# Input sums at fixed steps, a shortened last norm, and two shared first outputs in a hybrid encoder step

## The chip, the cores and the metric

The kernel runs on one core of one Trainium2 chip. A core has TensorE (PE in the profile, its weight loads PEld), VectorE (DVE), ScalarE (ACT), GpSimd (POOL) and SyncE (SP), each with its own instruction queue that runs in order, and 16 DMA engines. The metric is the device time of one execution in microseconds; the time of a kernel is the median of its runs. Loads and stores are issued by SP, additions into memory by DMA from POOL.

## The reference

One layer on 576 tokens (512 prompt, 64 sample) of width 2048, in float32. Conditioning gives shifts, scales and gates; then one input projection, two kinds of attention, an output projection, a post-norm, a squared-ReLU MLP of width 8192 and the last post-norm. What matters here is the second half:

```python
x = layer_norm(ALPHA * x + g_a * jnp.einsum('bse,ed->bsd', mix, w_out), ln_mix_g, ln_mix_b)
u = (_norm(x) * (1.0 + sc_m) + sh_m).astype(x.dtype)
h = jnp.square(jax.nn.relu(jnp.einsum('bsd,df->bsf', u, w_up) + b_up))
x = layer_norm(ALPHA * x + g_m * jnp.einsum('bsf,fd->bsd', h, w_down), ln_mlp_g, ln_mlp_b)
```

The result also holds the keys, values and log forget values; the change does not touch them.

## The kernel before

Activations lie transposed: 128 partitions are 128 of the 2048 features, and a block row of `big`, `ahi` and `alo` is 16 such blocks by 576 tokens. Every float32 product is made as three reduced ones: an operand is split into a high part (a copy by ScalarE to the narrower type: `whi`, `shi`, `ahi`, `th`) and a low part (the difference, by VectorE: `wlo`, `slo`, `alo`, `tl`), and high x high, high x low and low x high are added. So each weight piece costs ScalarE one copy and VectorE one subtraction before TensorE can use it.

The order of work is written out by hand. `em` is the emitter: TensorE's loop calls `em.tick()` once per step (in a plain product a step is one input block, that is three matmuls; 16 steps are one output block), and a tick puts out whatever is due. `em.after(n, fn)` makes `fn` due n steps later; generators in `em.side` and `em.back` advance by one `yield` per step, one behind the other. `em.drain()` puts out all that is left at once. Since each engine's queue runs in order, the step at which an instruction is put out decides what it stands behind.

The tokens go in two groups: A is columns 256 to 576, B is columns 0 to 256. The stages that the change touches:

*Up blocks of group B.* After the mixer's post-norm, 12 of the 64 blocks of the up projection are made plainly (`up_block`, `proj`): 16 steps per block, the weights in pieces of half a block that SP loads to `raw` (three buffers, refilled when a piece's `wlo` is done), split two pieces ahead in `take()` (L160, L161). `up_block` ends in a relu on ScalarE (L1015), 3 steps later the square on VectorE (L1018), then a store `hd` by SP; for blocks 8 to 11 a negated copy `nrelu` on ScalarE (L1020) and its store `nd` follow. The remaining 52 blocks use sums of inputs and of weights, seven products in place of eight. The input sums are made beside group B's up blocks by the generator `input_sums`: for each of 8 pairs of feature blocks it loads the pair from `ud` to `x32` (L1054, two buffers, two pairs ahead), makes two differences at once (L1062), a third (L1064) and a fourth sum (L1066) in a tile `sums`, copies the high parts on ScalarE (L1070, L1071) and subtracts the low parts on VectorE (L1073, L1075). A pair takes 18 steps.

*The turn.* Behind the last up block come `Sums`: the weight pieces of the seven-product stages, loaded to `sraw`, added (`add`, L1108 to L1112) and split (`make`, L1128, L1129) four ahead. The old pools are closed, and the first `make(4)` stands before the first matmul.

*The end.* The last four hidden blocks are multiplied plainly for all 16 outputs: `down_last(k, cols)` makes outputs 2k and 2k+1 for the given token columns, in four steps each (`four_blocks`, L1324 to L1326), and `gated` adds them to `big`. All 16 are made for group A, then all 16 for group B with the kept weights. `stats` gathers mean and variance by transposes beside it. Group A's last norm, `final_norm`, runs beside group B's products: `ln_finish` makes mean and inverse root (a power on POOL) and spreads them by a matmul with a diagonal; then eight pairs of blocks are normalised (L1436: subtract, multiply), by VectorE for groups 2, 8 and 14 and by POOL for the others, scaled by ScalarE (`affine`, L1426) and stored (`y_out`, L1431). Group B's, `final_last`, stands at the very end.

The pools lie on a left and a right stack; a tile waits for the earlier tiles whose memory it takes.

Of the kernel before, what the change touches and what calls it, by code (L numbers as in the profile page):

```python
# [172 lines left out]
def program(tc, xT, cT, cr, wad0, wad1, bada, win0, win, wf, bf, rel, ck, cv, clogf, wout0, wout, wup, bup, wst, lnv,  # L173
# [3 lines left out]
    with ExitStack() as ctx:  # L177
# [832 lines left out]
        def up_block(f, cols):  # L1010
            ps = new_acc()
            proj(ahi, alo, cols, ps)
            (a, b), = cols
            r = rl.tile([P, NT], F32, tag="relu", name=f"relu{f}_{a}", bufs=2)[:, a:b]
            S.activation(r, ps[:, 0, : b - a], AF.Relu, bias=bupc[:, f : f + 1])  # L1015

            def square():
                V.tensor_tensor(r, r, r, ALU.mult)  # L1018
                if f in nd:
                    S.mul(n, r, -1.0)  # L1020

            if f in nd:
                n = rl.tile([P, NT], F32, tag="nrelu", name=f"nrelu{f}_{a}")[:, a:b]
            em.after(3, square)
            em.after(7, lambda: nc.sync.dma_start(hd[f][:, a:b], r))
            if f in nd:
                em.after(8, lambda: nc.sync.dma_start(nd[f][:, a:b], n))
# [18 lines left out]
        def input_sums():  # L1046


            xs = {}

            def load(p):
                if p < 8:
                    x = xs[p] = xt.tile([P, 4, HN], F32, tag="x32", name=fresh("x32"), bufs=2)
                    nc.sync.dma_start(x.rearrange("p (a b) c -> p a (b c)", b=2), ud[p])  # L1054

            load(0)
            load(1)
            yield from wait(12)
            for p in range(8):
                x = xs.pop(p)  # L1060
                t = xt.tile([P, 4, HN], F32, tag="sums", name=fresh("sums"))
                V.tensor_tensor(t[:, 0:2], x[:, 0:4:3], x[:, 1:2].to_broadcast([P, 2, HN]), ALU.subtract)  # L1062
                yield from wait(3)
                V.scalar_tensor_tensor(t[:, 2], t[:, 0], -1.0, x[:, 3], ALU.mult, ALU.subtract)  # L1064
                yield from wait(3)
                V.scalar_tensor_tensor(t[:, 3], t[:, 2], -1.0, x[:, 2], ALU.mult, ALU.subtract)  # L1066
                load(p + 2)
                yield from wait(1)
                h1, l1 = (v[:, 2 * p, HN:] for v in (ahi, alo))
                S.copy(h1, t[:, 0])  # L1070
                S.copy(th[:, p], t[:, 1:])  # L1071
                yield from wait(5)
                V.tensor_tensor(l1, t[:, 0], h1.bitcast(F32), ALU.subtract)  # L1073
                yield from wait(3)
                V.tensor_tensor(tl[:, p], t[:, 1:], th[:, p].bitcast(F32), ALU.subtract)  # L1075
                yield from wait(3)
# [4 lines left out]
        class Sums:  # L1081
# [33 lines left out]
            def make(self, upto):  # L1115
                while self.made < min(upto, self.n):
# [4 lines left out]
                    if q in self.places:  # L1121
                        hi, lo = self.places[q]
                    else:
                        hi, lo = (
                            self.pool.tile([P, 7, P], F32R, tag=t, name=f"{t}{q}", bufs=4)[:, : raw.shape[1]]
                            for t in ("shi", "slo")
                        )
# [25 lines left out]
        sums.pool_raw.append(srx.enter_context(tc.tile_pool(name="sr2", bufs=1, reuse_waits="tile")))  # L1153
        sums.load()

        swx = ExitStack()
        sw = swx.enter_context(tc.tile_pool(name="sw", bufs=1, side="right", reuse_waits="tile"))
        sums.pool = sw
        sums.make(4)
        z = sw.tile([P, 7, HN], F32, name="z")  # L1160
# [7 lines left out]
        UP, DOWN = (0, 2, 5, 4, 1, 6, 3), (1, 3, 6, 4, 2, 0, 5)  # L1168
# [237 lines left out]
        with tc.tile_pool(name="fl", bufs=1, side="right", reuse_waits="tile") as flp:  # L1406
# [13 lines left out]
            def affine(eng, g, a, b):  # L1420

                for kb in (g, g + 1):
# [16 lines left out]
            def final_norm(tiles, a, b):  # L1439

                yield from wait(6)
                yield from ln_finish(mp, stf, mur1, tiles, new_tr, EPS / ALPHA**2, 6)
                for g in range(0, KB, 2):
                    eng = V if g in (2, 8, 14) else G
# [3 lines left out]
                    affine(S, g, a, b)  # L1448
                    y_out(g, a, b)

            def final_last(tiles, a, b):
# [4 lines left out]
                dg = mp.tile([P, 2, n, P], F32, name="dg_last")  # L1456
                ps = new_acc()[:, :, : n * P]
# [5 lines left out]
                for j in range(2):  # L1463
                    for i in range(n):
                        V.tensor_scalar(dg[:, j, i], ident, mv[:, i, 0:1] if j == 0 else rs[:, i : i + 1], None, ALU.mult)
                    T.matmul(ps[:, j], ones, dg[:, j].rearrange("p a b -> p (a b)"), start=True, stop=True)
                    S.copy(mur[:, j], ps[:, j])
                mine, other = [0, 2, 6, 8, 12, 14], [4, 10]
                for g in other:
                    for _ in norm_pair(G, g, a, b, [mur[:, j] for j in range(2)]):  # L1470
                        pass
                    affine(G, g, a, b)
                work = [norm_pair(V, g, a, b, [ps[:, j] for j in range(2)]) for g in mine]
                next(work[0])
                for i, g in enumerate(mine):
# [3 lines left out]
                    affine(S, g, a, b)  # L1479
# [9 lines left out]
            for k in range(8):  # L1489
                down_last(k, GROUP_B)  # L1490
# [111 lines left out]
```

## Time and profile before

| | |
|---|---|
| time, median of 3 runs | 2587.33 us (2587.07 to 2587.91) |
| the profiled execution | 2590.35 us |
| its span | 2588.6 us |
| mean granted TensorE clock | 0.991 |
| TensorE busy | 2526.0 us, 98% |
| VectorE, ScalarE, POOL busy | 82%, 44%, 13% |
| DMA moved | 483.56 MB |
| up blocks of group B | 1154.8 to 1241.6 us |
| products and norms of the end | 2500 to 2588.6 us |

All times in the text are microseconds from the span's start. In the answers of the profile a row of instructions reads: start, duration, engine, line of the kernel, operation, written <- read, shape, count, and in brackets the idle time ahead of it and what ended it. A row of waits reads: engine, tile and line <- what it waited for: total, times, longest.

### The profile page before, as it was taken

How to read it: one execution, taken by the hardware profiler on the slowest of the kernel's cores; microseconds unless marked ns; L12 is line 12 of the kernel's file. 1: busy time of each engine (PE TensorE's matmuls, PEld its weight loads, DVE VectorE, ACT ScalarE, POOL GpSimd, SP SyncE). 2: the span in 40 equal slices, each digit the busy share in tenths (PEclk: the TensorE clock that was granted, in tenths of full speed). 3: DMA queues.
4: the chain of work that ended last, by engine and by line, in shares of the span. 5: the costliest groups of instructions: out<-in, count | busy, mean ns of one | idle time of the engine just before them, and what ended most of it. 6: DMA issues, size and time to landing. Idle time of an engine off the chain costs nothing.

```text
span 2588.6 us, 48474 instructions
## 1 busy us (share of the span) xinstructions
PE 2526.0 (98%) x19235; PEld 2481.8 (96%) x19235; DVE 2126.7 (82%) x3740; ACT 1133.0 (44%) x1787; POOL 328.1 (13%) x373
## 2 busy tenths in 40 slices
PE   7999999999999999998999999999999999999996
PEld 5899999999999999998999999999999999999996
DVE  5668989898899558876788888888788988888886
ACT  2243333333333424764444444444555555555552
POOL 0021121232332200000000000000011111111114
PEclk8999999999999999999999999999999999999998
DMA  9845667656666544667555444444866666666662
GB/s 368 326 145 181 238 208 232 217 197 219 200 207 218 184 144 159 212 190 236 160 161 157 132 136 144 146 145 140 268 170 176 181 165 173 177 172 155 192 170 74
DMA packets 188819, 483.56 MB, mean 187 GB/s; under 512 B 16728, under 2 KB 49304, under 8 KB 187568
## 3 DMA queue, kind: packets, MB, share of 16 engines
q1 hardware_dynamic: 167728, 456.57, 53.6%
q0 software_dynamic: 20864, 23.89, 6.0%
q8 instruction: 151, 2.47, 0.4%
q14 instruction: 76, 0.62, 0.1%
HBM read 408.07 MB, written 57.77 MB: 180 GB/s over the span
## 4 chain that ended last, share of the span: by engine, by line
PE 83%; DVE 5%; issue 4%; DMA 3%; POOL 3%; ACT 1%; SPq 0%; ACTq 0%; POOLq 0%; DVEq 0%
PE acc L222 18%; PE q L1176 13%; PE q L1177 13%; PE q L1175 13%; PE acc L224 9%; PE tr L1176 2%; PE tr L1177 2%; PE tr L1175 2%; DVE junk L770 1%; DMA ada<-in_wad 1%; PE acc L1325 1%; PE acc L1324 1%; PE acc L1326 1%; PE tr L443 1%; DVE wlo L161 1%
## 5 line engine op out<-in xcount | busy, mean ns | idle before, releaser
L1128 ACT CAST shi<-sraw 128x896 fp32r<-128x896 f32 (+1 forms) x448 | 416.7, 931 | 468.3 <-PE q L1176 283.4
L222 PE MATMUL acc<-ahi,whi 128*128 128x288 f32 (+2 forms) x2384 | 603.7, 303 | 3.7 <-ACT whi L160 2.9
L224 PE MATMUL acc<-ahi,wlo 128*128 128x288 f32 (+2 forms) x2384 | 583.0, 295 | 9.0 <-DVE wlo L161 9.0
L222 PE MATMUL acc<-alo,whi 128*128 128x288 f32 (+2 forms) x2384 | 582.6, 294 | 0.0
L1129 DVE TENSOR_TENSOR slo<-sraw,shi 128x896 fp32r<-128x896 f32 (+1 forms) x448 | 475.9, 1072 | 46.7 <-ACT shi L1128 40.7
L222 PEld LDWEIGHTS acc<-ahi,whi 128*128 128x128 f32 x2384 | 406.3, 189 | 14.7 <-issue 5.7
L224 PEld LDWEIGHTS acc<-ahi,wlo 128*128 128x128 f32 x2384 | 409.5, 188 | 11.0 <-DVE wlo L161 11.0
L222 PEld LDWEIGHTS acc<-alo,whi 128*128 128x128 f32 x2384 | 409.2, 189 | 0.5 <-DVE alo L957 0.2
L770 DVE CUSTOM_DVE_ANT_0 junk<-ada,cb 128x512 f32<-128x512 f32 x512 | 367.2, 717 | 36.7 <-DMA ada<-in_wad 25.9
L1177 PE MATMUL q<-ahi,slo 128*128 128x288 f32 x1296 | 383.2, 296 | 0.0
L1176 PE MATMUL q<-tl,shi 128*128 128x288 f32 x1296 | 383.0, 296 | 0.0
L1175 PE MATMUL q<-th,shi 128*128 128x288 f32 x1296 | 382.0, 295 | 0.4 <-DVE z L1192 0.4
L1176 PE MATMUL q<-alo,shi 128*128 128x288 f32 x1296 | 382.1, 295 | 0.0
L1175 PE MATMUL q<-ahi,shi 128*128 128x288 f32 x1296 | 381.2, 294 | 0.4 <-DVE z L1190 0.4
L1177 PE MATMUL q<-th,slo 128*128 128x288 f32 x1296 | 381.2, 294 | 0.0
L161 DVE TENSOR_TENSOR wlo<-raw,whi 128x1024 fp32r<-128x1024 f32 x208 | 256.7, 1237 | 104.4 <-ACT whi L160 103.1
L160 ACT CAST whi<-raw 128x1024 fp32r<-128x1024 f32 x208 | 216.9, 1047 | 117.5 <-PE acc L222 97.3
L1175 PEld LDWEIGHTS q<-th,shi 128*128 128x128 f32 x1296 | 243.9, 188 | 1.2 <-issue 0.8
L1175 PEld LDWEIGHTS q<-ahi,shi 128*128 128x128 f32 x1296 | 243.9, 188 | 0.7 <-DVE z L1190 0.7
L1176 PEld LDWEIGHTS q<-alo,shi 128*128 128x128 f32 x1296 | 244.1, 188 | 0.0
L1177 PEld LDWEIGHTS q<-th,slo 128*128 128x128 f32 x1296 | 243.9, 188 | 0.0
L1177 PEld LDWEIGHTS q<-ahi,slo 128*128 128x128 f32 x1296 | 243.7, 188 | 0.0
(299 smaller groups left out, 4045.9 us busy)
## 6 DMA issues: line engine op xcount, KB each, us to landing
sraw<-in_wst SPq DMA_DIRECT2D x232, 512.0 KB, 4.4
ada<-in_wad SPq DMA_DIRECT2D x192, 512.0 KB, 5.9
raw<-in_win SPq DMA_DIRECT2D x96, 512.0 KB, 4.4
raw<-in_wout SPq DMA_DIRECT2D x64, 512.0 KB, 3.7
hp<-z SPq DMA_DIRECT2D x26, 1008.0 KB, 6.9
raw<-in_wup SPq DMA_DIRECT2D x48, 512.0 KB, 4.4
big<-z POOLq DMA_DIRECT2D x74, 288.0 KB, 5.1
alo<-hp SPq DMA_DIRECT2D x34, 576.0 KB, 6.0
```

The lines of the kernel that those rows point to most:

```text
L160: nc.scalar.copy(hi, raw)
L161: nc.vector.tensor_tensor(lo, raw, hi.bitcast(F32), ALU.subtract)
L222: T.matmul(o, whi, x[:, kb, a:b], start=start and x is hi, stop=False, **kw)
L224: T.matmul(o, wlo, hi[:, kb, a:b], start=False, stop=stop, **kw)
L443: T.matmul(ps[32 * k : 32 * k + 32, : 2 * P], cst[:, 4 * i + k, :], raw[:, k, :], start=i == 0, stop=i == 3,)
L770: V.tensor_tensor_reduce(junk, raw[:, k], cb[:, v], 1.0, 0.0, ALU.mult, ALU.add, parts[:, 2 * l + k, v, q : q + 1],)
L1128: S.copy(hi, raw)
L1129: V.tensor_tensor(lo, raw, hi.bitcast(F32), ALU.subtract)
L1175: T.matmul(out, wh, xh, start=start, stop=False)
L1176: T.matmul(out, wh, xl, start=False, stop=False)
L1177: T.matmul(out, wl, xh, start=False, stop=stop)
L1324: T.matmul(out, w[0][:, j], hi[:, a:b], start=j == 0, stop=False)
```

## The change

- The negated copy of a relu goes from step 3 (behind the square) to step 9, its store from 8 to 12.
- `input_sums` is no generator any more: all its pieces are put out by `em.after` at fixed steps, a pair every 19. Pair p is loaded at step 19p-4, summed at 12, 14 and 16, copied at 25, and its low parts follow at 30 and 32. There are three `x32` tiles, and the sums are written over them (the third and fourth change places, hence `UP`).
- No drain ahead of the last up block; `sums.add` of the first weights is put out 13 steps into it. The split weights lie in one tile for high and low part, in other pools; the first split piece and `z` have a pool of their own.
- Group A's last norm starts without the 6 waits and with 3 in place of 6 in its finish; VectorE takes groups 2, 6 and 10.
- Group B's last norm has a tile and an accumulator each for mean and scale, the last pair's scaling is shared by ScalarE and VectorE, and the stores of POOL's groups come later.
- Outputs 0 and 1 of the last four blocks are made for both groups at once, with group A's.

```diff
             def square():
                 V.tensor_tensor(r, r, r, ALU.mult)
-                if f in nd:
-                    S.mul(n, r, -1.0)
...
             if f in nd:
-                em.after(8, lambda: nc.sync.dma_start(nd[f][:, a:b], n))
+                em.after(9, lambda: S.mul(n, r, -1.0))
+                em.after(12, lambda: nc.sync.dma_start(nd[f][:, a:b], n))
...
+            xs, todo = {}, []
+            for i in (0, 2, 1):
+                xt.tile([P, 4, HN], F32, tag=f"x32_{i}", name=fresh("x32"))
             for p in range(8):
...
+                def load(p=p):
+                    xs[p] = xt.tile([P, 4, HN], F32, tag=f"x32_{p % 3}", name=fresh("x32"))
+                    nc.sync.dma_start(xs[p].rearrange("p (a b) c -> p a (b c)", b=2), ud[p])
...
+                def fourth(p=p):
+                    x = xs[p]
+                    V.scalar_tensor_tensor(x[:, 2], x[:, 3], -1.0, x[:, 2], ALU.mult, ALU.subtract)
+
+                def high(p=p, h1=h1):
+                    S.copy(h1, xs[p][:, 0])
+                    S.copy(th[:, p], xs[p][:, 1:])
...
+                for n, fn in ((-4, load), (12, both), (14, third), (16, fourth), (25, high), (30, low1), (32, low3)):
+                    todo.append((max(19 * p + n, 0), len(todo), fn))
+            for n, _, fn in sorted(todo):
+                em.after(n + 1, fn)
...
-                        hi, lo = (
-                            self.pool.tile([P, 7, P], F32R, tag=t, name=f"{t}{q}", bufs=4)[:, : raw.shape[1]]
-                            for t in ("shi", "slo")
-                        )
+                        hl = self.pools[q % 4 > 0].tile([P, 2, 7, P], F32R, tag=f"shl_{q % 4}", name=f"shl{q}")
+                        hi, lo = (hl[:, i, : raw.shape[1]] for i in range(2))
...
-        em.side.append(input_sums())
+        input_sums()
         for f in range(FP):
             if f == FP - 1:
-                em.drain()
                 xtx.close()
...
                 sums.load()
                 sums.load()
+                em.after(13, sums.add)
             up_block(f, GROUP_B)
         em.drain()
-        sums.add()
...
-        UP, DOWN = (0, 2, 5, 4, 1, 6, 3), (1, 3, 6, 4, 2, 0, 5)
+        UP, DOWN = (0, 2, 6, 4, 1, 5, 3), (1, 3, 6, 4, 2, 0, 5)
...
             def final_norm(tiles, a, b):
-                yield from wait(6)
-                yield from ln_finish(mp, stf, mur1, tiles, new_tr, EPS / ALPHA**2, 6)
+                yield from ln_finish(mp, stf, mur1, tiles, new_tr, EPS / ALPHA**2, 3)
                 for g in range(0, KB, 2):
-                    eng = V if g in (2, 8, 14) else G
+                    eng = V if g in (2, 6, 10) else G
...
-                dg = mp.tile([P, 2, n, P], F32, name="dg_last")
-                ps = new_acc()[:, :, : n * P]
+                dg = [mp.tile([P, n, P], F32, name=f"dg_last{j}") for j in range(2)]
+                ps = [new_acc()[:, 0, : n * P] for _ in range(2)]
...
-                    affine(S, g, a, b)
-                    if i in (0, 3):
+                    affine((S, V if i + 1 == len(work) else S), g, a, b)
+                    y_out(g, a, b)
+                    if i in (1, 4):
                         y_out(other[i // 3], a, b)
-                    y_out(g, a, b)
 
             for k in range(8):
-                down_last(k, GROUP_A)
+                down_last(k, (*GROUP_A, *GROUP_B) if k == 0 else GROUP_A)
...
             for k in range(8):
-                down_last(k, GROUP_B)
+                if k > 0:
+                    down_last(k, GROUP_B)
```

More of the change, by code (lines that the diff above doesn't have):

```diff
@@ L1046, in input_sums @@
         def input_sums():
[L1049 to L1058, printed above, removed]
-            for p in range(8):
[L1060 to L1068, printed above, removed]
-                h1, l1 = (v[:, 2 * p, HN:] for v in (ahi, alo))
[L1070 to L1076, printed above, removed]
@@ L1147, in program @@
                 sums.load()
+                em.after(13, sums.add)
             up_block(f, GROUP_B)
         em.drain()
-        sums.add()
         rlx.close()
         wpx.close()
-        sums.pool_raw.append(srx.enter_context(tc.tile_pool(name="sr2", bufs=1, reuse_waits="tile")))
+        swx = ExitStack()
+        right = lambda name, x=srx: x.enter_context(tc.tile_pool(name=name, bufs=1, side="right", reuse_waits="tile"))
+        s3 = right("s3")
+        sums.pool_raw.append(right("sr2"))
+        sw = right("sw", swx)
+        sums.pools = [sw, s3]
+        z = sw.tile([P, 7, HN], F32, name="z")
         sums.load()
-        swx = ExitStack()
-        sw = swx.enter_context(tc.tile_pool(name="sw", bufs=1, side="right", reuse_waits="tile"))
-        sums.pool = sw
         sums.make(4)
-        z = sw.tile([P, 7, HN], F32, name="z")
         forms = [
@@ L1418, in down_last, with affine @@
                     gated(m, outs, cols)
-            def affine(eng, g, a, b):
-                for kb in (g, g + 1):
+            def affine(engs, g, a, b):
+                for kb, eng in zip((g, g + 1), engs):
                     zz = big[:, kb, a:b]
@@ L1447, in final_norm @@
                         yield
-                    affine(S, g, a, b)
+                    affine((S, S), g, a, b)
                     y_out(g, a, b)
@@ L1464, in final_last @@
                     for i in range(n):
-                        V.tensor_scalar(dg[:, j, i], ident, mv[:, i, 0:1] if j == 0 else rs[:, i : i + 1], None, ALU.mult)
-                    T.matmul(ps[:, j], ones, dg[:, j].rearrange("p a b -> p (a b)"), start=True, stop=True)
-                    S.copy(mur[:, j], ps[:, j])
+                        V.tensor_scalar(dg[j][:, i], ident, mv[:, i, 0:1] if j == 0 else rs[:, i : i + 1], None, ALU.mult)
+                    T.matmul(ps[j], ones, dg[j].rearrange("p a b -> p (a b)"), start=True, stop=True)
+                    S.copy(mur[:, j], ps[j])
                 mine, other = [0, 2, 6, 8, 12, 14], [4, 10]
@@ L1471, in final_last @@
                         pass
-                    affine(G, g, a, b)
-                work = [norm_pair(V, g, a, b, [ps[:, j] for j in range(2)]) for g in mine]
+                    affine((G, G), g, a, b)
+                work = [norm_pair(V, g, a, b, ps) for g in mine]
                 next(work[0])
@@ L1478, in final_last @@
                     next(work[i])
-                    affine(S, g, a, b)
-                    if i in (0, 3):
+                    affine((S, V if i + 1 == len(work) else S), g, a, b)
+                    y_out(g, a, b)
+                    if i in (1, 4):
                         y_out(other[i // 3], a, b)
-                    y_out(g, a, b)
             for k in range(8):
-                down_last(k, GROUP_A)
+                down_last(k, (*GROUP_A, *GROUP_B) if k == 0 else GROUP_A)
                 if k % 2 == 1:
```

10 lines of the change are left out of this document (added).

## The prediction

> **What bounds the kernel now.** I read the busy table of the page first, then busy times by stretches of time (columns: the stretch, its length, busy us and instructions of PE, PEld, DVE, ACT and POOL, granted clock, DMA share, GB/s), then the waits and the order of instructions in the stretches where TensorE is not full.
>
> ```profile
> PE 2526.0 (98%) x19235; PEld 2481.8 (96%) x19235; DVE 2126.7 (82%) x3740; ACT 1133.0 (44%) x1787; POOL 328.1 (13%) x373
> ```
> ```profile
> 1840.00:2400.00 560.00, 560.00 (x4230) 559.69 (x4229) 480.91 (x665) 307.39 (x466) 71.28 (x62) 1.00 0.66 175
> ...
> 2500.00:2572.00 72.00, 66.34 (x502) 64.81 (x501) 53.05 (x106) 18.38 (x36) 21.50 (x13) 0.98 0.26 74
> ```
> ```profile
> 1154.80:1241.60 86.80, 74.81 (x578) 71.47 (x576) 56.63 (x79) 41.89 (x61) 0.00 (x0) 0.96 0.70 220
> 1178.80:1230.20 51.40, 43.90 (x338) 41.46 (x337) 37.57 (x56) 25.66 (x36) 0.00 (x0) 0.97 0.72 225
> 1230.20:1241.50 11.30, 11.30 (x98) 11.29 (x96) 5.23 (x6) 4.16 (x7) 0.00 (x0) 1.00 0.43 132
> ```
>
> The reader is to see that the whole kernel is TensorE at full clock except in three places that the change touches: 1154.8 to 1241.6 (the up blocks of group B, beside which the input sums are made), the turn right after it, and the end from about 2566 on. No matmul is removed, so only idle time there can be won. The last row gives the free pace: 96 matmuls in 11.30 us are 0.118 us each, so one step (three matmuls) is 0.353 us and a block of 16 steps 5.65 us. Twelve blocks would be 67.8 us and take 86.8. Blocks 3 to 9 fill the middle row (seven blocks of 48 matmuls, 336 of its 338): 39.6 us at free pace, in 51.4, so 11.8 us are lost there; blocks 0 to 2 (1154.8 to 1178.8) lose 24.0 - 17.0 = 7.0; the last two, with the sums done, lose nothing.
>
> The waits between 1154 and 1246:
>
> ```profile
> DVE wlo L161 <- ACT whi L160: 21.1, 11, 2.3
> ACT th L1071 <- DVE sums L1066: 11.4, 8, 2.0
> ...
> PE acc L224 <- DVE wlo L161: 9.0, 10, 2.8
> DVE sums L1062 <- DMA x<-ud: 5.1, 1, 5.1
> ```
>
> and one turn of the wheel, from VectorE's and ScalarE's order of time:
>
> ```profile
> 1205.94 1.23 DVE L161 TENSOR_TENSOR wlo<-raw,whi 128x1024 fp32r<-128x1024 f32 x1 [2.29 <-ACT whi L160]
> ...
> 1211.17 0.46 DVE L1066 SCALAR_TENSOR_TENSOR sums<-sums,x 128x288 f32<-128x288 f32 x1
> 1213.92 1.23 DVE L161 TENSOR_TENSOR wlo<-raw,whi 128x1024 fp32r<-128x1024 f32 x1 [2.29 <-ACT whi L160]
> ```
> ```profile
> 1211.66 0.92 ACT L1071 CAST th<-sums 128x864 fp32r<-128x864 f32 x1 [1.56 <-DVE sums L1066]
> 1212.48 0.47 ACT L1015 ACTIVATE relu<-acc,bupc 128x256 f32<-128x256 f32 x1
> 1212.85 1.98 ACT L160 CAST whi<-raw 128x1024 fp32r<-128x1024 f32 x2
> ```
>
> VectorE works from 1205.94 to 1211.63, then stands 2.29 us: its next weight part needs whi, whi stands on ScalarE behind the copy th, and th, issued one step after the fourth sum, waits for that sum. The engines take turns instead of overlapping: 7.98 us for a block of 5.65. Neither is full (37.57 and 25.66 us of 51.4).
>
> **The change, part by part.**
>
> *Sums at fixed steps.* The copy now follows the fourth sum by 9 steps (3.2 us) and the first low part follows the copy by 5. VectorE may run 3.2 us late before ScalarE feels it, so the 2.29 us stand goes. What is late next? VectorE's own work: 37.57 us for these seven blocks with a pair every 18 steps; at 19 steps, with the sums a little under half of it, some 0.9 less, 36.7 us against 39.6. That fits. DMA work is 0.72 x 51.4 = 37.0 us: that fits too. ScalarE has the same copies, in place of a separate sums tile the sums are written over x, at the same number of elements: nothing. Moving the negated copy from step 3 to 9 and its store from 8 to 12 lets ScalarE pass the square that it waits for; it exists for four of the twelve blocks only, and the SP queue then meets a store whose source is ready: nothing. The loads are the cost. Before, pair p+2 was requested at the fourth sum of pair p, about 30 steps before its use; now a pair is requested 16 steps ahead, on the SP queue that also carries raw weights and hd stores:
>
> ```profile
> DMA to landing us min/median/max: 5.3/6.0/6.8
> ```
>
> This is for the eight x loads. 16 steps are 5.65 us; 6.0 and about 0.4 to issue are 6.4, so VectorE waits about 0.7 us with the next wlo behind it, seven times: 4.9 us. Its spare time is 39.6 - 36.7 = 2.9, so about 2.5 us of the wait reaches TensorE, since part of the spare time is not where it is needed. Blocks 3 to 9: 39.6 + 2.5 = 42.1, gain **9.3**. Bounds: 0 (the wheel only finds another partner) and 11.8 (free pace).
>
> *The first sum* keeps its place: load at step 1, use at step 13, in both kernels, so blocks 0 to 2 keep their 7.0. That the second load no longer goes out with it could bring the landing to the shortest, 5.3: at most 0.6. I take nothing.
>
> *The turn.*
>
> ```profile
> 1241.73 0.47 ACT L1015 ACTIVATE relu<-acc,bupc 128x256 f32<-128x256 f32 x1 [3.75 <-PE acc L224]
> ...
> 1242.69 0.42 ACT L1020 ACTIVATE nrelu<-relu 128x256 f32<-128x256 f32 x1 [0.49 <-DVE relu L1018]
> ...
> 1244.22 1.78 ACT L1128 CAST shi<-sraw 128x896 fp32r<-128x896 f32 x2 [1.10 <-DVE sraw L1112]
> 1245.21 0.61 PE L1175 MATMUL tr<-ahi,shi 128*128 128x288 f32 x1 [3.51 <-ACT shi L1128]
> ```
>
> The weight sums now come at step 13 of the last block, three steps (1.06 us) before its end, their loads at its start instead of behind the drained work. ScalarE's copy shi then stands only behind the negated relu (to 1243.11), not behind the sums (1244.22): TensorE restarts **1.0** us earlier, with a gap of 2.5 instead of 3.51. The first shi tile lies in the new layout on raw weights that are long split, so it waits for no store. Bounds: 0 (sraw lands late) and 1.0, without the clock.
>
> The clock is the open part:
>
> ```profile
> 1171.00:1174.00 3.00, 2.21 (x13) 2.22 (x14) 1.43 (x3) 1.41 (x2) 0.00 (x0) 0.76 0.36 115
> 1174.00:1177.00 3.00, 3.00 (x20) 3.00 (x19) 2.52 (x3) 1.76 (x3) 0.00 (x0) 0.67 0.96 295
> ...
> 1246.00:1249.00 3.00, 2.72 (x12) 2.67 (x12) 2.92 (x6) 1.17 (x2) 0.00 (x0) 0.50 0.50 175
> 1249.00:1252.00 3.00, 3.00 (x17) 3.00 (x16) 2.93 (x5) 1.03 (x2) 0.00 (x0) 0.65 0.50 145
> 1252.00:1255.00 3.00, 3.00 (x25) 3.00 (x24) 2.79 (x5) 1.47 (x2) 0.00 (x0) 1.00 0.44 106
> ```
>
> After the turn 29 matmuls pass in 6 us instead of 50: 21 x 0.12 = 2.5 us lost. But the longest wait of PE above, 2.8 us, comes just ahead of the first two of these rows, and there the clock fell to 0.76 and 0.67 as well. A gap of 2.5 lies near that, so I give nothing. The Trainium skill, "TensorE: Matmul & The Clock Gate", section "Why this matters for your kernels", says that idle gaps up to about 3 us between bursts leave the clock up; by it the turn would gain 3.5 instead of 1.0. This case's 2.8 us gap speaks against it, so it has a small chance below.
>
> *The middle* (split weights hi and lo in one tile, other addresses): same instructions under a TensorE that is full (560.00 of 560): nothing, bounds -1 and +1.
>
> *The end.*
>
> ```profile
> 2553.43 19.00 POOL L1436 TENSOR_TENSOR big<-big,mur 128x640 f32<-128x640 f32 x10 [8.95 <-ACT mur L323]
> 2572.53 0.70 POOL L1462 TENSOR_TENSOR rs_last<-rs_last,mhalf 128x2 f32<-128x2 f32 x1
> ```
> ```profile
> 2566.04 3.39 DVE L1436 TENSOR_TENSOR big<-big,mur 128x640 f32<-128x640 f32 x2
> ...
> 2576.72 7.26 DVE L1436 TENSOR_TENSOR big<-big,acc 128x512 f32<-128x512 f32 x12 [2.98 <-ACT mur L1467]
> ```
> ```profile
> 2575.06 1.22 PE L1466 MATMUL acc<-dg_last,ones 128*128 128x256 f32 x2 [0.95 <-ACT mur L1467]
> ```
> ```profile
> L1431 SPq DMA_DIRECT2D out_yT<-big x16: 372/373/429, 2558.5 to 2585.5; - x16
> ```
>
> Group A's norm on POOL ends at 2572.43, and the power for group B's last norm stands behind it in the same queue: that sets the end. Group A's products end later by two blocks of twelve 256-wide matmuls, 24 x 0.118 = 2.8 us. The norm then starts earlier by the 6 waits removed and by 12 within its finish (6 + 6 + 6 + 6 steps become 3 + 3 + 3 + 3): 18 x 0.353 = 6.4. Net 3.6 earlier: the ten operations, still ten and beside the same six VectorE ones, run 2549.9 to 2568.9. VectorE's pair of 3.39 us moves from the last place (group 14) to group 10, ahead of group B's end, so its statistics are ready by then too. From POOL's end to VectorE's norm it is 4.3 us now (2572.43 to 2576.72), because mean and scale share one accumulator and the first subtraction waits for both. With two accumulators it needs only the mean: 1.22 for the matmul and, as an estimate from ScalarE's 0.42 for a 256-wide copy, 0.5 for the two 128-wide diagonals, about 1.8. Start 2570.7 instead of 2576.7: 6.0. The last affine pair shared by ScalarE and VectorE saves one of ScalarE's, about 0.5. POOL's own two pairs end about when VectorE's last does, and their store goes ahead of it. Gain **6.5**; bounds 3.5 (only POOL's start counts) and 7.5. Products of the first two outputs for both groups are the same matmuls: nothing.
>
> Sum: 9.3 + 1.0 + 6.5 = 16.8. The profiled span 2588.6 becomes 2571.8, its execution of 2590.35 becomes 2573.5; the runs' median, 3.0 below that execution, becomes **2570.5**.
>
> **The rivals.**
>
> 1. *Only the end is won.* The wheel finds a new partner (raw weight buffers that come free late), blocks 3 to 9 keep 51.4. For it: three raw buffers, each refilled only after a wlo. Against: DMA has 37.0 us of work in 51.4. Gain 1.0 + 6.5: **2579.8**.
> 2. *Free pace, and the clock kept at the turn*: 11.8 + 3.5 + 6.5 = 21.8, **2565.5**. For it: VectorE's 36.7 of 39.6. Against: 6.0 us landings on 5.65 us notice.
> 3. *Slower: each x load stalls as the first does now.* The first costs TensorE 2.8 us and then 16 matmuls of slow clock (33 instead of 56 from 1171 to 1177, less 0.79 us idle), 1.9 us: 4.7. Seven more are 32.9 against the 11.8 lost now: 21.1, less 7.5, is 13.6 slower, **2600.9**. It decides from (11.8 + 7.5) / 7 = 2.8 us a load; that needs a landing near 8.5 us, and the longest seen is 6.8.
> 4. *No change*: the sums win nothing and POOL's end does not move, because the doubled first blocks push group A back as far as the waits bring it forward; only the turn is left, 1.0 at most: **2586.3**.
>
> **How the numbers follow.** Forecast (2564 to 2577) 0.60, rival 1 0.15, rival 2 0.13, rival 4 0.07, rival 3 0.05. About 0.2% (5.2 us) is what a measurement of this kernel can tell from no change. Faster: 0.60 + 0.15 + 0.13 = 0.88; same 0.07; slower 0.05. All bounds at their best (11.8, 0.6, 3.5, 1, 7.5) make 24.4 and 2562.9; the range 2563 to 2580 reaches from there over the forecast and rivals 1 and 2 and leaves out the 0.12 of the others.
>
> **What would show it.** Right: blocks of 5.7 to 6.3 us in the input-sum stage, hardly a wait of wlo on whi, VectorE's waits now on x loads; a gap of about 2.5 us at the turn; POOL's ten norm operations ending before 2569 less what was won earlier, and VectorE's last norm within 2 us behind. Wrong: blocks that stay at 7 to 8 us, x loads with waits over 2 us, or POOL still 3 us behind group B's statistics.

## The result, and the profile after

The changed kernel takes 2575.03 us (median of 5 runs, 2574.03 to 2579.54); the kernel before, 2587.91 in the same comparison. The ratio is 0.9948 (95% interval 0.9937 to 0.9959), a gain of 12.9 us, between 10.6 and 16.3 by the interval. Forecast were 2570.5 and a gain of 16.8, with a range of 2563 to 2580. The profiled execution took 2578.5 us, its span 2576.8, that is 11.8 less than the profiled span before.

The busy table of the changed kernel, then its busy times by stretches (columns as in the prediction):

```profile
PE 2522.5 (98%) x19235; PEld 2480.1 (96%) x19235; DVE 2125.9 (83%) x3741; ACT 1133.2 (44%) x1786; POOL 328.3 (13%) x373
```
```profile
1154.07:1233.65 79.58, 71.58 (x578) 69.70 (x576) 55.32 (x79) 40.38 (x58) 0.00 (x0) 0.98 0.73 240
```
```profile
1177.72:1220.65 42.93, 40.91 (x338) 39.89 (x337) 32.02 (x46) 23.26 (x31) 0.00 (x0) 1.00 0.79 260
1220.65:1233.65 13.00, 11.58 (x98) 11.33 (x96) 8.88 (x13) 5.11 (x9) 0.00 (x0) 1.00 0.54 192
```

The same matmuls, and the 12 up blocks of group B in 79.58 us instead of 86.71: blocks 3 to 9 in 42.93 instead of 51.40, but the last two in 13.00 instead of 11.30. The waits between 1150 and 1250:

```profile
ACT whi L160 <- DMA raw<-in_wup: 14.2, 8, 3.3
DVE x L1061 <- DMA x<-ud: 11.8, 5, 4.8
DVE wlo L161 <- ACT whi L160: 10.4, 8, 3.5
...
ACT th L1073 <- DVE x L1069: 6.7, 5, 1.7
PE acc L224 <- DVE wlo L161: 6.6, 6, 2.6
ACT nrelu L1025 <- DVE relu L1018: 4.6, 2, 2.6
ACT nrelu L1025 <- DMA nd<-nrelu: 4.5, 3, 3.2
```

The main reading rests on one more pair of rows, ScalarE's wait ahead of each pair's two copies, before (between 1154 and 1246) and after:

```profile
ACT ahi L1070 <- DVE sums L1062: 24.2, 8, 6.1
```
```profile
ACT ahi L1072 <- DVE x L1061: 3.8, 3, 1.4
```

This wait for the sums fell from 24.2 to 3.8 us, that of `wlo` for `whi` from 21.1 to 10.4, that of `th` for the fourth sum from 11.4 to 6.7; the wait for x grew from 5.1 (once) to 11.8 (five times). ScalarE now also waits for a DMA that was in no row before: `nrelu` for its own last store. The x waits one by one, and the landing of the eight loads:

```profile
1168.22 0.76 DVE L1061 TENSOR_TENSOR x<-x 128x576 f32<-128x576 f32 x1 [4.80 <-DMA x<-ud]
...
1182.59 0.76 DVE L1061 TENSOR_TENSOR x<-x 128x576 f32<-128x576 f32 x1 [1.63 <-DMA x<-ud]
...
1199.22 0.76 DVE L1061 TENSOR_TENSOR x<-x 128x576 f32<-128x576 f32 x1 [2.64 <-DMA x<-ud]
...
1212.21 0.76 DVE L1061 TENSOR_TENSOR x<-x 128x576 f32<-128x576 f32 x1 [1.40 <-DMA x<-ud]
...
1221.18 0.76 DVE L1061 TENSOR_TENSOR x<-x 128x576 f32<-128x576 f32 x1 [1.35 <-DMA x<-ud]
```
```profile
DMA to landing us min/median/max: 5.9/6.8/7.5
```

The turn, by ScalarE's, VectorE's and TensorE's order of instructions, and the clock after it:

```profile
1235.24 0.42 ACT L1025 ACTIVATE nrelu<-relu 128x256 f32<-128x256 f32 x1 [0.92 <-DMA nd<-nrelu]
1235.57 1.76 ACT L1134 CAST shl<-sraw 128x896 fp32r<-128x896 f32 x2
```
```profile
1233.17 0.69 DVE L1116 TENSOR_TENSOR sraw<-sraw 128x512 f32<-128x512 f32 x1 [2.41 <-DMA sraw<-in_wst]
...
1234.70 0.42 DVE L1018 TENSOR_TENSOR relu<-relu 128x256 f32<-128x256 f32 x1
```
```profile
1236.54 0.61 PE L1181 MATMUL tr<-ahi,shl 128*128 128x288 f32 x1 [2.73 <-ACT shl L1134]
```
```profile
1237.00:1240.00 3.00, 2.72 (x12) 2.37 (x12) 2.93 (x5) 1.16 (x2) 0.00 (x0) 0.50 0.59 175
1240.00:1243.00 3.00, 3.00 (x14) 3.00 (x14) 2.92 (x6) 1.02 (x3) 0.00 (x0) 0.50 0.44 127
1243.00:1246.00 3.00, 3.00 (x24) 3.00 (x23) 2.82 (x4) 1.03 (x2) 0.00 (x0) 0.95 0.33 117
```

The gap is 2.73 us instead of 3.51, and the clock behind it is as low as before. The end, by POOL and VectorE, with one row of the beginning of that stretch:

```profile
2543.50 19.16 POOL L1442 TENSOR_TENSOR big<-big,mur 128x640 f32<-128x640 f32 x10 [4.05 <-ACT mur L323]
2562.76 0.69 POOL L1467 TENSOR_TENSOR rs_last<-rs_last,mhalf 128x2 f32<-128x2 f32 x1
```
```profile
2564.26 7.33 DVE L1442 TENSOR_TENSOR big<-big,acc 128x512 f32<-128x512 f32 x12 [0.29 <-ACT mur L1472]
2571.63 0.41 DVE L1434 TENSOR_SCALAR big<-big,lnc 128x256 f32<-128x256 f32 x1
```
```profile
2511.18 1.30 DVE L288 BATCH_NORM_STATS2 stt<-tr 128x6 f32<-128x512 f32 x2 [1.56 <-DMA big<-z]
```
```profile
2511.93 0.66 PE L287 MATMUL tr<-ident,big 128*128 128x128 f32 x4 [1.43 <-DVE stt L288]
```

POOL's ten operations end at 2562.66, VectorE's last norm starts 1.6 us behind them (4.3 before). Group B's mean and variance were ready at 2561.67, so POOL now holds the last norm up by a microsecond at most. The last two rows are a wait that was not there before: group A's statistics wait for a DMA that reads `z`, and TensorE stands 1.43 us for them.

For all kernels below two lengths are compared, each read from one profile: *up to the turn*, from the first matmul of group B's up blocks to the first seven-product matmul, and *the end*, from the first plain 320-wide product of the last blocks to the end of the span. Ratios are to the kernel before, in the same comparison, with 95% intervals.

| kernel | ratio | up to the turn, us | end, us |
|---|---|---|---|
| before | 1 | 90.39 | 84.53 |
| changed | 0.9948 (0.9937 to 0.9959) | 82.47 | 80.31 |
| e1_sums_only | 0.9980 (0.9971 to 0.9989) | 84.09 | 84.61 |
| e9_last_norms | 0.9984 (0.9976 to 0.9993) | 90.36 | 79.29 |
| e2_end_only (changed, products apart) | 0.9975 (0.9963 to 0.9987) | 83.36 | 81.91 |
| e3_copy_at_17 | 0.9974 (0.9963 to 0.9984) | 86.77 | 79.93 |
| e4_load_early | 0.9950 (0.9936 to 0.9964) | 79.59 | 79.99 |
| e5_sums_later | 0.9938 (0.9925 to 0.9950) | 77.11 | 80.49 |
| e6_stats_off_z | 0.9947 (0.9935 to 0.9959) | 81.31 | 79.09 |
| e8_apart_off_z | 0.9950 (0.9936 to 0.9963) | 81.60 | 79.26 |
| e10_two_nrelu | 0.9936 (0.9924 to 0.9948) | 77.09 | 80.17 |
| e14_negated_at_3 | 0.9962 (0.9950 to 0.9975) | 83.97 | 79.79 |
| e13_together | 0.9934 (0.9922 to 0.9947) | 75.52 | 79.16 |
| e12_without_pool | 0.9919 (0.9906 to 0.9933) | 73.47 | 78.63 |

An interval is some 6 us wide, so effects of 1 to 3 us are read from the two lengths. Where the code is the same they agree within 0.7 us at the end (79.8 to 80.5 in the six kernels that have the change's) and within 2 up to the turn (82.47, 83.36, 81.31 and 81.60 in the change, e2, e6 and e8). Shorter pieces vary more: in these four, blocks 3 to 9 take 42.45 to 45.60 us and the gap at the turn is 2.69 to 3.32 us; the code of before has a gap of 3.51 us in its own profile and of 4.61 in that of e9_last_norms. The middle, 1259 us of the same work, varied between 1258.1 and 1261.8 without order, so the 1.1 us by which it is longer after the change says nothing.

### The profile page after: what moved, and what is told of

The parts are those of the page before. It is cut to its first block, busy times and chain, and to the rows that moved or that the text cites. A ratio compares the mean times of both kernels' runs of the same rounds, so it can differ in the third digit from the quotient of the medians.

```text
span 2576.8 us, 48159 instructions
## 1 busy us (share of the span) xinstructions
PE 2522.5 (98%) x19235; PEld 2480.1 (96%) x19235; DVE 2125.9 (83%) x3741; ACT 1133.2 (44%) x1786; POOL 328.3 (13%) x373
## 5 line engine op out<-in xcount | busy, mean ns | idle before, releaser
L1134 ACT CAST shl<-sraw 128x896 fp32r<-128x896 f32 (+1 forms) x448 | 416.7, 931 | 482.8 <-PE q L1183 310.3
L1135 DVE TENSOR_TENSOR shl<-sraw,shl 128x896 fp32r<-128x896 f32 (+1 forms) x448 | 476.2, 1073 | 51.6 <-ACT shl L1134 46.2
L1182 PE MATMUL q<-alo,shl 128*128 128x288 f32 x1296 | 384.6, 297 | 0.0
L1181 PE MATMUL q<-th,shl 128*128 128x288 f32 x1296 | 383.6, 296 | 0.5 <-DVE z L1198 0.4
L1182 PE MATMUL q<-tl,shl 128*128 128x288 f32 x1296 | 382.8, 295 | 0.0
L1183 PE MATMUL q<-ahi,shl 128*128 128x288 f32 x1296 | 382.7, 295 | 0.0
L1183 PE MATMUL q<-th,shl 128*128 128x288 f32 x1296 | 382.4, 295 | 0.0
L1181 PE MATMUL q<-ahi,shl 128*128 128x288 f32 x1296 | 381.2, 294 | 0.0
L1181 PEld LDWEIGHTS q<-th,shl 128*128 128x128 f32 x1296 | 244.0, 188 | 1.4 <-issue 0.9
L1183 PEld LDWEIGHTS q<-ahi,shl 128*128 128x128 f32 x1296 | 244.5, 189 | 0.0
L1181 PEld LDWEIGHTS q<-ahi,shl 128*128 128x128 f32 x1296 | 244.4, 189 | 0.0
L1183 PEld LDWEIGHTS q<-th,shl 128*128 128x128 f32 x1296 | 244.4, 189 | 0.0
L1182 PEld LDWEIGHTS q<-tl,shl 128*128 128x128 f32 x1296 | 244.1, 188 | 0.0
```

Of the source, the lines that this page charges most:

```text
L1134: S.copy(hi, raw)
L1135: V.tensor_tensor(lo, raw, hi.bitcast(F32), ALU.subtract)
L1181: T.matmul(out, wh, xh, start=start, stop=False)
L1182: T.matmul(out, wh, xl, start=False, stop=False)
L1183: T.matmul(out, wl, xh, start=False, stop=stop)
```

## The experiments

**The fixed steps alone.** The kernel before with the new `input_sums` and the moved negated copy; turn and end stay as they were.

```diff
-        em.side.append(input_sums())
+        input_sums()
...
-                em.after(8, lambda: nc.sync.dma_start(nd[f][:, a:b], n))
+                em.after(9, lambda: S.mul(n, r, -1.0))
+                em.after(12, lambda: nc.sync.dma_start(nd[f][:, a:b], n))
```

> The kernel before with the input sums at fixed steps (and the negated copy at step 9) alone. Theory (in the changed kernel the stage of group B's up blocks fell from 86.7 to 79.5 us, because ScalarE's copy no longer stands one step behind the fourth sum): the stage falls by 7 us, the turn and the end stay (gap about 3.6 us, end 84.5 us from the first plain product on), so 7 us faster than before, ratio about 0.9973. Rival (the drain removed ahead of the last up block and the early weight sums are part of that gain): 4 us or less.

Ratio 0.9980, 5.2 us. In the profile the twelve blocks take 79.02 us, 7.7 less than before and as in the change, so what this stage won is the steps' doing. The time is between the theory's 7 us and the rival's 4. The gap at the old turn is longer than in the profile before (3.51):

```profile
1234.17 0.61 PE L1183 MATMUL tr<-ahi,shi 128*128 128x288 f32 x1 [4.91 <-ACT shi L1136]
```

The old turn does its loads, adds and splits behind the last block, so part of what the stage wins may be spent there; one profile doesn't show it, since the same turn had a gap of 4.61 us in e9_last_norms. Against 84.09 us here, 81.3 to 83.4 with the change's code: by these profiles the new turn is worth 0.7 to 2.8 us once the stage is fast, which is little above the spread.

**The last norms alone.** The kernel before with the new `final_norm`, `affine` and `final_last`.

```diff
-                yield from wait(6)
-                yield from ln_finish(mp, stf, mur1, tiles, new_tr, EPS / ALPHA**2, 6)
+                yield from ln_finish(mp, stf, mur1, tiles, new_tr, EPS / ALPHA**2, 3)
...
-                    eng = V if g in (2, 8, 14) else G
+                    eng = V if g in (2, 6, 10) else G
```

> The kernel before, with the new last norms alone (final_norm without its six waits and with three steps instead of six, six of its norm operations on VectorE at groups 2, 6, 10, two accumulators and the shared affine in final_last); the first two outputs of the last blocks stay apart for the two token groups. Theory: with no doubled products group A's statistics come 2.8 us earlier than in the changed kernel, POOL's ten operations end near 2566 on the scale of the profile before, the end is then set by group B's own statistics, and the end stretch falls from 84.5 to 80 or 81 us; time 3.5 to 4.5 us less than before. Rival: POOL still ends behind group B's statistics, end stretch 81 to 82 with POOL's power directly behind its last norm operation. Rival: the end is not set by POOL at all, end stretch stays at 84 to 85, time as before.

Ratio 0.9984, 4.1 us; the end falls from 84.53 to 79.29.

```profile
2546.41 19.19 POOL L1436 TENSOR_TENSOR big<-big,mur 128x640 f32<-128x640 f32 x10 [3.61 <-ACT mur L323]
2569.31 0.70 POOL L1461 TENSOR_TENSOR rs_last<-rs_last,mhalf 128x2 f32<-128x2 f32 x1 [3.71 <-DVE rs_last L1460]
```

POOL is done at 2565.6 and then waits 3.71 us for group B's statistics: it no longer sets the end. Theory met, a little better than its 80 to 81. From here group B's own statistics set it, so a POOL that is done still earlier would win nothing more here.

**The doubled products undone.** The next kernel is the changed one with the first two outputs of the last blocks made for the groups apart, all else as in the change. The text on record under this label speaks of another kernel, the one that e9_last_norms is, and by that run it is missed: POOL ended 6.7 us earlier (6.4 expected), but the gain was 4.1 us and not 6.5 to 7.

```diff
-                down_last(k, (*GROUP_A, *GROUP_B) if k == 0 else GROUP_A)
+                down_last(k, GROUP_A)
```

> The kernel before with the two last norms changed (waits, engines, two accumulators, shared last scaling), but the products of the two groups kept apart. Theory (POOL's end and the shared accumulator set the end; the doubled outputs only push group A back): POOL ends 6.4 us earlier than before, group B's statistics then come last, VectorE's last norm starts about 2570.3 instead of 2576.7, 6.5 to 7 us faster, ratio about 0.9974. Rival (the doubled outputs are needed for the gain): 4 us or less.

```profile
2505.86 1.30 DVE L288 BATCH_NORM_STATS2 stt<-tr 128x6 f32<-128x512 f32 x2 [2.53 <-DMA big<-z]
```

The wait for the DMA that reads `z` grows from 1.56 to 2.53 us and the end from 80.31 to 81.91. So the doubled products, which put group A's first statistics later, cover part of this wait. The ratio, 0.9975, is 7 us from the change's; the two lengths show 2.5 of it. The profiled execution, 2576.28 us, was the fastest of its seven (median 2581.59), so the lengths come from one that lost less than most; where the others lost the rest is not known. The next two kernels ask what the wait is for, and whether covering it is all that the doubled products do.

```diff
-            mp, stf, mur1 = ln_tiles(flp)
+            mp, mur1 = flp, flp.tile([P, 2, NT], F32, name="mur1f")
+            stf = flp.tile([P, 5, 4, 6], F32, name="sttf")
```

> The changed kernel, with the tile of the last statistics placed behind the tile of means, so that it no longer lies on the memory of z. Theory: TensorE's wait of 1.4 us in the last blocks (its transpose behind VectorE, VectorE behind z's accumulating DMA) goes, all behind it comes 1.4 us earlier, the end stretch falls from 80.3 to about 78.9 us. Rival: the wait is for z's sum itself and not for the memory, then it stays at 1.3 us or more.

> The changed kernel with the first two outputs of the last blocks made for the two token groups apart again, and with the last statistics' tile off the memory of z. Theory: the doubled products only cover the wait for z's accumulating DMA; without that wait they win nothing, so the end stretch is 79 to 79.5 us, as with them and without the wait (79.1), and 2.6 us less than apart with the wait (81.9); time as in e6_stats_off_z, 2573.5 to 2576. Rival: they win something of their own, then the end stretch is 80.5 us or more.

Both theories hold. With the statistics off the memory of `z` no wait for that DMA is left in either profile, and the end is 79.09 us with doubled products and 79.26 without. The wait was for memory, 1.2 us at the end; the doubled products win nothing but its cover. The times (0.9947 and 0.9950) can't tell 1 us from nothing.

**The copy's distance.** The changed kernel with the high copy one step behind the fourth sum, as near as it was before.

```diff
-... (25, high), (30, low1), (32, low3)):
+... (17, high), (22, low1), (24, low3)):
```

> The changed kernel with the copy put out one step behind the fourth sum (17) and the low parts at 22 and 24, as far behind as before the change; all else as changed. Theory (the distance between sum and copy is what broke the alternation): VectorE waits for whi again by 15 us or more, blocks 3 to 9 back to 49 us or more from 42.9, so 6 to 8 us slower than the changed kernel, about 2582. Rival (the pace of 19 steps, three tiles, or the loads did it): blocks 3 to 9 stay within 1 us of 42.9, about 2575.

Ratio 0.9974 against 0.9948, the intervals apart: 6.7 us slower than the change. Its waits between 1150 and 1250:

```profile
ACT ahi L1072 <- DVE x L1061: 25.4, 8, 5.8
DVE wlo L161 <- ACT whi L160: 15.4, 8, 2.5
```

ScalarE again stands for the sums ahead of each pair's copies, 25.4 us in all, with `whi` behind them and `wlo` waiting for `whi`. So the distance between the sum and its copy is a mechanism of this gain: the time is that of the theory, and the wait of `ahi` is as long again as before the change (25.4 and 24.2 us, against 3.8). The blocks alone don't show it. Blocks 3 to 9 took 45.7 us, not the 49 or more of the theory, and e2_end_only has 45.6 with the change's steps; the last two took 15.9, with the loss in block 10, where the first negated copy stands. The twelve blocks give back 4.7 of the 7.1 us that they had won; what won the rest was not tried apart. This one edit takes back about half of the time that the whole change won.

**Earlier x loads.** `(-4, load)` becomes `(-20, load)`.

> The changed kernel with each pair of input blocks loaded 20 steps ahead of its start instead of 4 (32 steps ahead of its first sum). Theory (the loads, 6.8 us to landing on 5.65 us of notice, are what is left of the loss): VectorE's waits for x fall from 11.8 us to the first one's 4.8, blocks 3 to 11 fall from 55.8 to about 52 us, 3 to 4 us faster than the changed kernel, about 2571.5. Rival (raw weights, for which ScalarE waits 14.2 us, are the ring that bounds the stage): blocks 3 to 11 stay at 55 us or more, about 2575.

```profile
DVE x L1061 <- DMA x<-ud: 5.1, 1, 5.1
```
```profile
1233.21 0.42 ACT L1025 ACTIVATE nrelu<-relu 128x256 f32<-128x256 f32 x1 [2.00 <-DMA nd<-nrelu]
```

The first row, of the waits: only the first load is still waited for, and the twelve blocks take 75.62 us, the last nine 52.3 as the theory has it. The second: at the turn the negated copy now stands 2.00 us for its one buffer, and the gap is 3.80 us. What is left, 2.9 us in the profile, is too small for this comparison: the time is that of the change, and the theory's 3 to 4 us are not seen in it.

**The sums 8 steps later**, with 4 more steps of notice: load at 19p - 8, first sum at 19p + 20, the rest as far behind it.

> The changed kernel with each x load requested 24 steps ahead of the first sum plus 4 (load at 19p - 8 instead of 19p - 4, sums and copies 8 steps later: first sum at 19p + 20). The very first load stays at step 0, its use moves from step 12 to step 20. Theory (x landing on short notice is what is left in the stage): VectorE's first wait for x falls from about 5 to about 2 us, TensorE's wait of 2.6 us in block 2 and the slow clock after it go, the later x waits go too; block 2 falls from 10.1 to 6 us or so, the stage from 79.6 to 73 to 75 us, time 2569 to 2572. Rival: time does not follow (2574 to 2576), because what is won in the stage is spent at the turn, where the negated relu waits for its one buffer: gap 4 us or more. Rival: the stall in block 2 is the weights' and not x's: block 2 stays near 10 us.

```profile
1156.51 0.47 ACT L1025 ACTIVATE nrelu<-relu 128x320 f32<-128x320 f32 x1 [3.00 <-DMA nd<-nrelu]
...
1226.96 0.42 ACT L1025 ACTIVATE nrelu<-relu 128x256 f32<-128x256 f32 x1 [3.01 <-DMA nd<-nrelu]
```
```profile
1160.00:1163.00 3.00, 3.00 (x18) 3.00 (x17) 1.78 (x3) 0.18 (x1) 0.00 (x0) 0.56 0.85 230
```

Block 2 falls from 10.06 to 5.65 us, the twelve blocks to 72.13, the ratio is 0.9938 (2572.58 us, just above the theory's 2572). The theory is right on block 2 and the stage, its first rival on the turn: the gap is 4.82 us. The two ScalarE rows show one tile on both sides of the stage: the negated copy of the last block of group A, ahead of block 1's weights, and that of the last of group B, ahead of the first sums' split. Each waits 3.0 us for the store before it. At the first of them TensorE stands twice, in the rows below, and then runs on a clock of 0.56 (the row above), so block 1 takes 8.31 us.

```profile
1157.97 0.39 PE L222 MATMUL acc<-ahi,whi 128*128 128x256 f32 x1 [1.00 <-ACT whi L160]
1159.23 0.39 PE L224 MATMUL acc<-ahi,wlo 128*128 128x256 f32 x1 [0.75 <-DVE wlo L161]
```

**Two buffers for the negated relu**, on top of the earlier loads.

```diff
-                n = rl.tile([P, NT], F32, tag="nrelu", name=f"nrelu{f}_{a}")[:, a:b]
+                n = rl.tile([P, 320], F32, tag="nrelu", name=f"nrelu{f}_{a}", bufs=2)[:, : b - a]
```

> The changed kernel with x loads at 19p - 20 instead of 19p - 4 (as in e4_load_early) and with two buffers for the negated relu instead of one. Theory: at the turn the negated relu no longer waits for the store before it (2.0 us in e4_load_early), so the gap falls from 4.0 us to 2.5 or less, the stage stays at 75 to 76 us, time 2571 to 2573. Rival: the gap stays at 3.5 us or more, because the weights' copies then wait for the loaded sums or for the split (sraw lands late).

Ratio 0.9936. The gap is 2.35 us instead of 3.80, the stage 74.59; theory met, its time (2572.87) at the upper end. Ahead of the stage the negated copy no longer waits for a store either: blocks 0 and 1 take 11.8 us, 13.3 with the earlier loads alone and 13.6 in the change.

**The negated copy back at step 3**, its store at 8, all else as in the change.

> The changed kernel with the negated copy back behind the square at step 3 and its store back at step 8. By the prediction this move costs and wins nothing: stage and gap together 81.3 to 82.5 us as in the changed kernel, time 2574 to 2576. Rival: ScalarE again stands behind the square in four of the twelve blocks with the weights' copies behind it; each of the four costs 0.5 us or more, stage and gap together 84 to 86 us, time 2577 to 2579.

Ratio 0.9962 against 0.9948, and up to the turn 83.97 us against 81.3 to 83.4. The place is clear where the sum is not: blocks 10 and 11 take 15.29 us, against 12.1 to 13.0 with the change's code, and the gap is 0.4 shorter. So the mechanism is the rival's, at about 2 us and not all of its 3; and it is not 0.5 us in each of four blocks, but one block, block 10 (9.63 us against 6.5 to 7.4). The price stands in one row of ScalarE:

```profile
1213.05 1.03 ACT L160 CAST whi<-raw 128x1024 fp32r<-128x1024 f32 x1
1219.09 0.42 ACT L1020 ACTIVATE nrelu<-relu 128x256 f32<-128x256 f32 x1 [5.01 <-DVE relu L1018]
1219.42 1.03 ACT L160 CAST whi<-raw 128x1024 fp32r<-128x1024 f32 x1
```

For 5.01 us ScalarE waits for a square that VectorE, itself late with x, has not reached; the next weight piece stands behind it.

**Together.** The later sums, two buffers, statistics off `z`; first with the negated copy on POOL, then with it on ScalarE.

> The changed kernel with four things of the experiments together: x loads at 19p - 8 and the sums 8 steps later (as in e5_sums_later), two buffers for the negated relu, the negated copy itself made on POOL instead of ScalarE, and the last statistics off the memory of z. Theory: stage 72 us as in e5_sums_later, gap at the turn 1.5 us (2.35 us with two buffers, less the copy of 0.42 and the wait ahead of it), end 79.1 us; together 9 us less than the changed kernel, time 2565 to 2569. Rival: POOL's copies beside VectorE make VectorE's operations longer (they took 1.8 instead of 0.8 us beside POOL at the end), the stage is 74 us or more and the time 2569.5 to 2572.

> As e13_together, but with the negated copy on ScalarE as in the changed kernel: x loads at 19p - 8, sums 8 steps later, two buffers for the negated relu, last statistics off the memory of z. Theory (POOL's copy of 0.85 us with its store and the raw weights queued behind cost e13_together part of its stage, and at the turn the loaded sums are late whoever makes the copy): stage 72 to 73 us, gap 2.4 to 2.8 us, end 79.1 us, time 2567 to 2570. Rival: what is left in the stage is raw weights that land late, with or without POOL: stage 73 us or more with ScalarE's weight copies waiting for raw weights, time 2570 to 2573 as in e13_together.

On POOL: 0.9934, 2571.59 us, the rival's side, with 72.8 us for the twelve blocks, between the two. The reason the rival gave is not enough: VectorE's operations kept their durations but for two low parts of weights beside one of POOL's copies (1.5 us each instead of 1.22). What grew in the waits, from 13.9 us in e5_sums_later, is this row:

```profile
ACT whi L160 <- DMA raw<-in_wup: 19.4, 13, 4.1
```

The gap was 2.53 us, not 1.5: at the turn the copy that was taken off ScalarE is replaced by a wait for the loaded sums, which VectorE adds only when they land:

```profile
1229.99 1.78 ACT L1134 CAST shl<-sraw 128x896 fp32r<-128x896 f32 x2 [0.98 <-DVE sraw L1120]
```

On ScalarE: 2567.82 us, ratio 0.9919, its interval below that of the change. The time is the theory's, the twelve blocks are shorter than its 72 to 73 us, and the gap, 3.02 us, is longer than its 2.4 to 2.8. The busy times of the twelve blocks:

```profile
1151.82:1222.11 70.29, 68.92 (x578) 68.05 (x576) 54.45 (x78) 40.45 (x57) 0.00 (x0) 1.00 0.80 264
```

70.29 us at a clock of 1.00, where free pace is 67.8. So this version is 7.5 us faster than the change by the ratios (0.9948 - 0.9919), and up to the turn and at the end 9.0 and 1.7 us shorter in the profile. That POOL's copy was to blame for the 2.5 us more in e13_together is not settled: raw weights were also waited for here (18.0 us), and one profile each can't tell a cause of that size from the landing of loads.

## Why the prediction was right, and where it was off

*The bound and the mechanism* were right: the time went out of the stage with the sums and out of the end, no matmul was saved, and the copy's distance from the sum won most of the stage (e3_copy_at_17). The size was too high: in the profile the twelve blocks won 7.1 us (9.3 forecast), the turn 0.8 (1.0) and the end 4.2 (6.5), 12.1 of 16.8. Of the signs of being right, the blocks and the norm's start came, and POOL's end was 1.4 us late; of the signs of being wrong, one x load waited 2.64 us and one of blocks 3 to 9 took 7.26. That TensorE is idle in three places only was too wide: before the change it also stands 14.7 us in the first 60 us and 8.7 between 400 and 1154.8, out of the change's reach. Nothing in the sum rests on it.

*Blocks 3 to 9*: forecast 42.1 us, measured 42.93. The term inside it was mis-sized: waits of 0.7 us on seven x loads, 4.9 in all. Four of the seven waited, for 1.35 to 2.64 us, 7.0 in all, because the loads landed in 6.8 us in the middle and not in 6.0 as before; DMA's share rose from 0.72 to 0.79 in these blocks. With earlier loads they took 40.8 us (e4_load_early), so by these two profiles the x waits cost TensorE about 2.2, forecast 2.5. It can be more: in e2_end_only, with the same steps, one load was waited for 3.92 us and TensorE stood 2.56 us behind it.

*Blocks 10 and 11* were the step that failed: "the last two, with the sums done, lose nothing", and "it exists for four of the twelve blocks only ... nothing" for the negated copy. With a pair every 19 steps the last sums reach into block 10. There the chain is x late, square late, ScalarE standing for the square ahead of the weights:

```profile
1223.28 0.42 ACT L1025 ACTIVATE nrelu<-relu 128x256 f32<-128x256 f32 x1 [2.63 <-DVE relu L1018]
```

They took 13.00 us instead of 11.30; with the x loads earlier, 11.5 (e4_load_early). Nor was the move of the copy worth nothing: without it these blocks lose about 2 us more (e14_negated_at_3).

*The first sum* kept its stall, as forecast: blocks 0 to 2 took 23.65 us (24.0), TensorE's longest wait 2.6 (2.8). Not seen was that some 1.5 us of this loss hang on the negated copy's single buffer (e10_two_nrelu against e4_load_early).

*The turn*: forecast 1.0 us and a gap of 2.5, measured 0.8 and 2.73, of which the spread of the same code leaves only the direction. The gap holds 0.92 us that the negated copy stands in the first row of the turn. VectorE adds the sums, which land at 1233.17, ahead of the square; and when the square is done at 1235.12, the copy's one buffer is still being stored. The prediction counted neither. The clock gave nothing, as forecast: after a gap of 2.73 us it was 0.50 for some 6 us. The Trainium skill, "TensorE: Matmul & The Clock Gate", section "Why this matters for your kernels", names idle gaps above about 3 us as what to avoid against throughput drops; here a drop followed a gap of 2.73 us, and the measurement decides.

*The end*: forecast 6.5 us, measured 4.2. The step from POOL's end to VectorE's last norm was right (1.8 forecast, 1.6 measured). Two things were missing. The statistics' new place on the memory of `z` put group A's norm later: 1.2 us (e6_stats_off_z; 1.1 between the means of the kernels with and without it). From the stretch's first product, POOL's ten ended 2.1 us earlier than before and not the 3.6 forecast; without that wait, 3.8. And the tail behind the start of the last norm, which the prediction made 0.5 shorter by sharing the last affine, came out longer. Before, it was 2588.6 - 2576.72 = 11.9 us; now it is 2576.8 - 2564.26 = 12.5. The sharing did its part: from the norm's start to the end of ScalarE's last affine it is 8.35 us instead of 8.78. But before, the last store went out 0.02 us behind that end; now it stands behind the store of POOL's second pair, which the change puts just ahead of it:

```profile
2572.61 0.97 SPq L1437 DMA_DIRECT2D out_yT<-big  x2
```

ScalarE ends at 2572.61, the last store is issued at 2573.14, and it lands 2.69 us later instead of 2.16. No run puts the two stores the other way round. These 1.1 and 1.2 us are the missing 2.3.

*The doubled products*: "nothing" was right for their matmuls and right by the end without the memory wait (79.09 and 79.26), but in this layout they are worth 1.6 us as a cover for it. The rivals: only the end won (e1_sums_only speaks against it), free pace (not reached; the x loads and the buffer stand in between), each load a stall (no), no change (no). The price of the third holds a slip: 6 us at 0.118 us a matmul are 51 and not 56, so the slow clock behind the first wait costs about 1.3 us and not 1.9, and that rival's time would be about 2597. It stays outside the range.

## What to carry to other kernels

An instruction that waits for another engine should be put into an in-order queue as far behind its source as the source may be late: one edit of that kind (copy at step 25 or 17 of a pair) carried half of this gain. When a stage becomes faster, look through every tile with one buffer and every tile that was moved: a wait that never showed, on a store or on a neighbour's memory, is what the new pace meets first. And add the lengths around the stage, since a wait won in it can come back at the next turn.

## What the runs showed of the hardware

The clock after short gaps. TensorE's first 6 us behind the restart in e10_two_nrelu, whose gap was 2.35 us:

```profile
1231.41:1233.41 2.00, 1.41 (x8) 1.17 (x9) 1.97 (x3) 0.79 (x1) 0.00 (x0) 1.00 0.66 160
1233.41:1235.41 2.00, 2.00 (x11) 2.00 (x10) 1.96 (x4) 1.37 (x2) 0.00 (x0) 0.51 0.44 168
1235.41:1237.41 2.00, 2.00 (x12) 2.00 (x12) 1.93 (x4) 0.41 (x1) 0.00 (x0) 0.64 0.43 105
```

The clock stayed at 1.00 for 2 us, then fell to 0.51 and was back within 6: after 2.73 us of gap it was at 0.50 from the start. So the drop can come after the work has begun again. Its length does not go by the gap alone. In e2_end_only, whose gap of 3.32 us is longer than both, the same three stretches behind the restart are:

```profile
1234.57:1236.57 2.00, 1.40 (x5) 1.17 (x6) 1.97 (x3) 0.79 (x1) 0.00 (x0) 0.66 0.66 155
1236.57:1238.57 2.00, 2.00 (x10) 2.00 (x10) 1.96 (x4) 1.38 (x2) 0.00 (x0) 0.50 0.44 169
1238.57:1240.57 2.00, 2.00 (x17) 2.00 (x17) 1.93 (x4) 0.40 (x1) 0.00 (x0) 0.99 0.40 115
```

All fourteen profiles have a drop at the turn, with gaps from 2.30 us up. It lasts 3.4 us in four of them (gaps of 2.30, 2.30, 2.35 and 3.32) and 6.8 in the other ten (2.53 to 4.91). What decides between the two is not shown.

Stores behind one another. In the last norm's stores of 256 columns, before and after, as far as their landing is on record, one that is issued within 0.8 us of the one ahead landed in 2.5 to 2.7 us, one that follows a microsecond or more behind in 2.2.

In six kernels with the same code ahead of them (the change, e2, e4, e5, e6 and e8) group B's up blocks start at 1150.7 to 1159.2 us. A gain of 3 us is not seen in such a time; two points inside one profile show it.
